# A two-layer hybrid decoder trunk on one core: where the conditioning products, the head norm, the low part and the spatial products stand in the order of work

## The chip, the cores and the metric

The kernel runs on one core of one Trainium2 chip. The metric is the device time of one execution in microseconds (us). The engines are TensorE (PE in the profile; its weight loads are PEld), VectorE (DVE), ScalarE (ACT), GpSimd (POOL) and SyncE (SP), which here issues nearly all DMAs from one queue, in program order.

## The reference

The input is x (256 tokens by 1024) and one conditioning vector c of 1024. Two layers follow, each of three sub-layers: a SwiGLU FFN (inner size 2816), a token mixer, a second FFN. The mixer of layer 0 is HGRN2, a gated linear recurrence with 8 heads of 128 in chunks of 64; the mixer of layer 1 is a gMLP with spatial gating over chunks of 128 tokens.

```python
def sublayer(x, fn, pre_g, post_g, shift, scale, gate, res_w):
    h = rms_norm(x, pre_g) * (1.0 + scale) + shift
    return x + res_w * gate * rms_norm(fn(h), post_g)

cond = silu(c)
mod = (cond @ ada_w[i] + ada_b[i]).reshape(B, 9, D_MODEL)   # shift, scale, gate of 3 sub-layers

def swiglu(h, w_in, w_out):
    a, b = split(h @ w_in, 2)
    return (silu(a) * b) @ w_out

# HGRN2: q, f, i, g = split(h @ w_in); log-decays b = cumsum(log f) in a chunk
#   scores[t, s] = sum_k q[t,k] k[s,k] exp(b[t,k] - b[s,k]) for s <= t, and a carried state
#   out = (rms_norm over each head(o) * out_norm * silu(g)) @ w_out
# gMLP: u, v = split(gelu(h @ w_in + b_in)); v = layer_norm(v)
#   out = (u * (tril(w_s[group]) @ v + b_s)) @ w_out
```

All is float32. The weights are some 280 MB that are read once.

## The kernel before

**Products in three parts.** Every weight block is read as float32, split into a high part (`hi`, a float32r cast on ACT, L122) and a low part (`lo` = raw - hi, a subtraction on DVE, L132), and activations are split in the same way; a product is hi*hi + hi*lo + lo*hi on PE. A block is 128 x 2048 and comes in two halves of 512 KB. `cast()` issues the half's load on SP and its cast on ACT, `sub()` its subtraction on DVE, `halves(n)` n of both. The halves land in a ring of four buffers (`raw`); a load waits on SP until the subtraction four halves earlier has freed its buffer. `next_block()` (called `nb`) hands out the next finished block and keeps `ahead` more finished.

**Conditioning products.** The 144 rows of conditioning weights (128 x 1024, 512 KB each) are not multiplied on PE: `ada()` loads one and multiplies and sums it against `cond` in one DVE instruction (L192). `pace(upto, blocks)` spreads the products that a stage owes evenly over so many weight blocks: after each block, `wblock()` adds `rate` to a credit and calls `ada` once for each whole credit. Loads go into a ring of three buffers, so the load of row j waits on SP for the product of row j - 3. Before, the load of row i + 2 is issued when product i is.

**The order.** Outside two kinds of region the framework's scheduler sets the order on each engine at compile time, by its own estimate of times and by a priority that is the place in the program; SP keeps program order. The text of the program is thus a wish: a DVE instruction that the scheduler thinks ready may be put ahead of earlier ones. Each engine then runs its list strictly in order. `paced()` ties the first matmul of a filler piece behind a given matmul (`self.gate`). Between `open()` and `close()` (the boundaries between sub-layers) the order on PE, DVE and ACT is that of the text. `self.hold` keeps casts, subtractions and conditioning products that come after a boundary behind the boundary's last instruction on ACT and DVE.

**The boundary** (`boundary`, between sub-layer s and s + 1): the last products of y in four pieces mm(t, h) of 18 matmuls (t: half of the tokens, h: half of the columns), after each piece a square with a row sum on ACT (`square`, L235), a multiplication by the gate on DVE (L319), the root of the mean (`inv_rms`: ACT L80, DVE reciprocal L248), `residual` (DVE L255, squares of the new x on ACT, `half_mean` L242 on DVE, which needs the first of these squares), then the norm's scaling, PE transposes (L271), `h_high` on ACT (L274), `h_full` (float32 h, DVE L287 or ACT L285) and `h_low` on DVE (L293). `go(0)`, 96 matmuls of the next sub-layer on the first tokens (L429), needs h_low from its 17th matmul on, for columns 4 to 7 from the 21st. A `plan` of four numbers says how many halves are cast and subtracted ahead of mm(0,0), after mm(0,0), around the first `residual` and around the second.

**The recurrence** (`hgrn`): feature products for q and f of heads 0-3, then for 4-7 (`feat`, 96 matmuls for two blocks, PE L460 to L462), `gate_f` on ACT and DVE, and for each half of the heads an attention `attn(hb)`: a diagonal product, seven levels (span 64 down to 1), each with two subtractions (L741, L746), an exp on ACT, a multiplication (L752), 16 matmuls (L758) and a masked copy on DVE (L729), and last the products with v (L791, L793). `zip_steps` hands PE one step of filler (`tok`: 12 matmuls for v or the gate g; `outs`) after each step of the attention. While attention 1 runs, `outs` does the head norm of attention 0 (`stats`: square on ACT L806, sums L814, gating L810, and `rsqrt`, nine small dependent DVE instructions L88 to L101), scales by r (L832), transposes on PE (`turn`, L836), splits, and multiplies by the output weights.

**The gMLP** (`gmlp`): for each of 12 units of 256 columns 48 matmuls for u (`unit`), four spatial products `vps` (L1050, two for each half k of the unit, all four into one PSUM bank), per half a gelu on ACT and two DVE instructions (L1055, L1057; L1057 reads vps), then 24 output matmuls.

Of the kernel before, what the change touches and what calls it, by code (L numbers as in the profile page):

```python
# [18 lines left out]
P = 128  # L19
# [14 lines left out]
class Body:  # L34
# [144 lines left out]
    def ada(self, upto):  # L179

        nc = self.nc
        while self.ada_next < min(upto, 144):
            i = self.ada_next
            for j in range(len(self.ada_tiles), min(i + (1 if self.ring else 3), 144)):
                if self.ring and j % 3:
                    t = self.p4.tile([P, D], F32, tag="t4", name="ada")
                else:
                    t = self.adap.tile([P, D], F32, tag="ada", name="ada")
                self.load(t, self.d["ada"][j])
                self.ada_tiles.append(t)  # L190
            t = self.ada_tiles[i]
# [59 lines left out]
    def residual(self, t, yg, r, st=None):  # L251

        for h in range(2):
# [5 lines left out]
            else:  # L259
                self.square(self.x[t][:, hs], st[0], h)  # L260
        if st is not None:
            self.half_mean(st)

# [45 lines left out]
    def boundary(self, y, G, mm, cols, table, plan=(4, 2, 0, 0)):  # L309


        nc = self.nc
# [23 lines left out]
        for _ in range(plan[2]):  # L336
            self.cast()
        self.residual(0, yg, r, sx)
        for _ in range(plan[2]):
            self.sub()  # L340
# [18 lines left out]
        gated(1, 1, yg1)  # L359
        r = self.inv_rms(sy1)  # L360
        for _ in range(plan[3]):
            self.cast()
        hf = self.h_full(1, pa1, cols, scalar=True)
        self.residual(1, yg1, r, sx1)
        for _ in range(plan[3]):
            self.sub()
        self.h_low(0, 1, hf)
        w = [[self.ready.pop(0) for _ in range(2)] for _ in range(2)]
# [275 lines left out]
    def hgrn(self, hT, G_fn, pre_next, nxt, bg):  # L644
        nc, tc = self.nc, self.tc
        self.pace(bg, 14)
        state = {}
# [180 lines left out]
        def turn(hb, u, og, r):  # L828
# [5 lines left out]
            for i in range(4):  # L834
                c0 = (i % 2) * S + (i // 2) * P
                nc.tensor.transpose(ps[:, c0:c0 + P], on[:, i, :], self.ident)  # L836
            return ps
# [79 lines left out]
        def products(i):  # L917
            wo = nb()
            return [lambda k=k, t=t, h=h: self.out_mm(y[t][h], t, h, oTs[i], k, wo, k, i + k == 0, False)
                    for k in range(2) for t in range(NT) for h in range(2)]  # L920

        def outs():
            og, r = stats(0, ops[0], False)
            for u in range(2):
                split(0, u, turn(0, u, og, r))
            yield
            y.extend(self.y_banks())
            for j, op in enumerate(products(0)):
                op()
                if j == 3:  # L930
                    yield
            yield

        y = []
        zip_steps(attn(1, bank_a, ops[1]), [
            tok(lambda t, ps: nc.scalar.copy(gg[:, t, 512:], ps)), outs()], 0)
        self.table("silu_and_others")
# [24 lines left out]
    def gmlp(self, hT, G_fn, pre_next, nxt, bg):  # L962
# [72 lines left out]
        for u in range(12):  # L1035
# [6 lines left out]
            for k in range(2):  # L1042
# [6 lines left out]
                for t in range(NT):  # L1049
                    nc.tensor.matmul(vps[:, k * S + t * P:k * S + (t + 1) * P], v[j // 2][:, j % 2, t, c0:c0 + P],  # L1050
                                     ws[:, g, :], start=True, stop=True)
                self.tact(z[:, k * S:(k + 1) * S], pu[:, k * S:(k + 1) * S], AF.Gelu_apprx_tanh,
                          bias=bcol[:, c:c + 1])
# [96 lines left out]
    def run(self):  # L1150
# [8 lines left out]
        subs = ["ffn0", "hg", "ffn1", "ffn2", "gm", "ffn3"]  # L1159
        tables = {"f": "silu_and_others", "h": "silu_and_others", "g": "gelu_apprx_tanh_and_others"}  # L1160
        bgs = {"ffn0": 40, "hg": 64, "ffn1": 92, "ffn2": 120, "gm": 138, "ffn3": 144}
        for s, kind in enumerate(subs):
# [10 lines left out]
            def nxt(y, G, mm, s=s, st=st):  # L1173
# [3 lines left out]
                else:  # L1177
                    if s != 1:
                        self.open()
                    self.boundary(y, G, mm, st["cols"], tables[subs[s + 1][0]], (2, 1, 1, 1) if s == 1 else (4, 2, 0, 0))  # L1180
                    self.hT = self.h2[:, 0], self.h2[:, 1]
# [111 lines left out]
```

## Time and profile before

| what | value |
|---|---|
| median of 3 runs | 1182.11 us (1179.4 to 1184.67) |
| the profiled execution | 1184.81 us, of which the span 1183.0 us |
| mean granted TensorE clock of it | 0.983 of full speed |
| instructions | 17089 |

The span is from the first to the last instruction. A busy PE is modelled and covers small gaps, so it is read here by its idle times and their releasers, and by the granted clock of a stretch, which has two levels, 1.2 GHz (0.50) and 2.4 GHz (1.00). The stages lie, by the trace, at about: FFN 0 from 15 to 205 us, boundary to the recurrence to 235, recurrence to 378, boundary to 402, FFNs 1 and 2 to 767, boundary, gMLP to 975, FFN 3 to the end.

### The profile page before, as it was taken

What the parts mean: (1) busy time and instruction counts of PE and PEld (TensorE: products, weight loads), DVE (VectorE), ACT (ScalarE), POOL (GpSimd) and SP (SyncE); (2) the same over time, 40 slices, a digit from 0 to 9 for tenths busy, and PEclk for the clock granted to TensorE, in tenths of its full rate; (3) what the DMA queues carried; (4) which work ended last, traced back from release to release, by engine and by line L of the source; (5) the groups of instructions that cost most, each with busy time, mean ns of one, the idle gap of its engine ahead of it and who ended that gap; (6) DMA issues with size and microseconds to landing.
All of it is one profiled execution on the core that took longest, in us unless ns stands there. A gap on an engine that the chain in (4) does not pass through costs nothing.

```text
span 1183.0 us, 17089 instructions
## 1 busy us (share of the span) xinstructions
PE 1141.4 (96%) x6518; PEld 995.8 (84%) x6518; DVE 904.7 (76%) x1379; ACT 666.3 (56%) x1046; POOL 6.8 (1%) x16
## 2 busy tenths in 40 slices
PE   7999999999969899999999999999999999999997
PEld 6989997898867788888888888888988988888886
DVE  6987867789987699886599986567887776866742
ACT  6554536769545665556566555555754367654631
POOL 0000000000000000000000000000000000000000
PEclk9999999998979899999999999999999999999999
DMA  9889988296255299887279988426777673766720
GB/s 351 309 315 334 334 286 274 82 356 223 95 183 186 87 344 366 320 309 228 93 257 367 342 313 278 151 81 230 279 265 247 241 248 104 241 230 223 237 101 36
DMA packets 79764, 282.31 MB, mean 239 GB/s; under 512 B 9873, under 2 KB 10561, under 8 KB 79682
## 3 DMA queue, kind: packets, MB, share of 16 engines
q1 hardware_dynamic: 78626, 278.05, 67.3%
q0 software_dynamic: 1056, 3.17, 0.9%
q8 instruction: 51, 0.84, 0.3%
q14 instruction: 31, 0.25, 0.1%
HBM read 280.11 MB, written 1.07 MB: 238 GB/s over the span
## 4 chain that ended last, share of the span: by engine, by line
PE 84%; DMA 5%; DVE 5%; ACT 3%; issue 1%; SPq 0%; DVEq 0%; ACTq 0%
PE ups L454 17%; PE pps L429 9%; PE ups L455 9%; PE y L163 8%; PE y L164 8%; PE y L162 8%; PE ups L574 4%; PE ups L462 3%; PE ups L460 3%; PE ups L461 3%; DMA ada<-in_ada 2%; PE ab L758 2%; DVE w L132 2%; DMA raw<-in_wgmu 2%; ACT w L122 1%
## 5 line engine op out<-in xcount | busy, mean ns | idle before, releaser
L132 DVE TENSOR_TENSOR w<-raw,w 128x1024 fp32r<-128x1024 f32 x376 | 453.4, 1221 | 95.6 <-ACT w L122 90.2
L122 ACT CAST w<-raw 128x1024 fp32r<-128x1024 f32 x376 | 387.4, 1048 | 175.4 <-DMA raw<-in_wffn 89.3
L454 PE MATMUL ups<-h,w 128*128 128x512 f32 x864 | 302.4, 393 | 0.0
L455 PE MATMUL ups<-h,w 128*128 128x256 f32 x864 | 242.1, 280 | 0.0
L192 DVE CUSTOM_DVE_ANT_0 ada<-ada,cond 128x1024 f32<-128x1024 f32 x144 | 174.1, 1219 | 24.9 <-DMA ada<-in_ada 24.9
L454 PEld LDWEIGHTS ups<-h,w 128*128 128x128 f32 x864 | 161.8, 187 | 36.9 <-issue 0.3
L162 PE MATMUL y<-w,t 128*128 128x512 f32 x448 | 178.8, 401 | 0.0
L163 PE MATMUL y<-w,t 128*128 128x512 f32 x448 | 177.3, 396 | 1.0 <-DVE w L132 1.0
L164 PE MATMUL y<-w,t 128*128 128x512 f32 x448 | 177.0, 396 | 0.0
L455 PEld LDWEIGHTS ups<-h,w 128*128 128x128 f32 x864 | 163.2, 189 | 1.0
L429 PE MATMUL pps<-w,h 128*128 128x512 f32 x480 | 116.7, 400 | 3.1 <-DVE h L293 3.1
L460 PE MATMUL ups<-h,w 128*128 128x256 f32 x416 | 118.6, 285 | 0.0
L462 PE MATMUL ups<-h,w 128*128 128x256 f32 x416 | 117.8, 283 | 0.0
L461 PE MATMUL ups<-h,w 128*128 128x256 f32 x416 | 117.6, 283 | 0.0
L429 PEld LDWEIGHTS pps<-w,h 128*128 128x128 f32 x480 | 91.0, 192 | 22.5 <-DVE h L293 3.5
L164 PEld LDWEIGHTS y<-w,t 128*128 128x128 f32 x448 | 84.3, 188 | 20.3
L163 PEld LDWEIGHTS y<-w,t 128*128 128x128 f32 x448 | 84.5, 189 | 19.2 <-DVE w L132 1.5
L162 PEld LDWEIGHTS y<-w,t 128*128 128x128 f32 x448 | 84.5, 189 | 18.8
L460 PEld LDWEIGHTS ups<-h,w 128*128 128x128 f32 x416 | 79.7, 192 | 1.1 <-issue 0.2
L461 PEld LDWEIGHTS ups<-h,w 128*128 128x128 f32 x416 | 79.7, 191 | 0.8 <-issue 0.2
L462 PEld LDWEIGHTS ups<-h,w 128*128 128x128 f32 x416 | 79.6, 191 | 0.0
L80 ACT ACTIVATE t<-t 128x256 f32<-128x256 f32 (+2 forms) x70 | 36.4, 522 | 45.4 <-DVE t L507 33.5
(198 smaller groups left out, 1317.1 us busy)
## 6 DMA issues: line engine op xcount, KB each, us to landing
raw<-in_wffn SPq DMA_DIRECT2D x264, 512.0 KB, 5.7
ada<-in_ada SPq DMA_DIRECT2D x144, 512.0 KB, 6.8
raw<-in_wgmu SPq DMA_DIRECT2D x48, 512.0 KB, 5.3
raw<-in_whg SPq DMA_DIRECT2D x40, 512.0 KB, 5.7
raw<-in_wgmv SPq DMA_DIRECT2D x24, 512.0 KB, 4.9
G<-gflat POOLq DMA_DIRECT2D x6, 512.0 KB, 5.8
t<-in_gbin SPq DMA_DIRECT2D x6, 256.0 KB, 5.7
x<-in_x SPq DMA_DIRECT2D x2, 512.0 KB, 4.2
```

What stands on the lines that cost most here:

```text
L122: self.after(self.nc.scalar.copy(hi[:, sl], raw), self.hold[0])
L132: self.after(self.nc.vector.tensor_sub(lo[:, sl], raw, hi[:, sl]), self.hold[1])
L162: self.paced(mm(ps, l[0], r[0], start=start, stop=False))
L163: mm(ps, l[0], r[1], start=False, stop=False)
L164: mm(ps, l[1], r[0], start=False, stop=stop)
L192: self.after(nc.vector.tensor_tensor_reduce(t, t, self.cond, 1.0, 0.0, ALU.mult, ALU.add, self.mod[i // 24][:, i % 24:i % 24 + 1]), self.h ...
L429: lambda g=g, i=i, j=j, kc=kc, w=w: mm(res[g][t], h2[:, i, t, kc, :], w, start=kc + i + j == 0, stop=i == 1 and kc == KC - 1)))
L454: self.paced(mm(ps, u[0], self.h2[:, :, :, kc, :], start=kc == 0, stop=False))
L455: self.last = mm(ps[:, 1, :], u[1], self.h2[:, 0, :, kc, :], start=False, stop=kc == KC - 1)
L460: self.paced(mm(o, u[0], h[0], start=start, stop=False))
L461: mm(o, u[0], h[1], start=False, stop=False)
L462: self.last = mm(o, u[1], h[0], start=False, stop=stop)
```

## The change

Five places change. (1) `ada` loads one row ahead of the product in place of two, in the same three buffers (except in the first eight blocks of FFN 0, which are not touched). (2) In the recurrence the 24 conditioning products are spread over 8 blocks in place of 14: three to a block. With the blocks that the boundary takes, these eight are handed out before attention 0 begins in the text. (3) The boundary's `half_mean` of the second residual moves behind `h_low`, the scalar `h_full` ahead of the casts and `h_low` ahead of the subtractions; the plan of boundary 0 goes from (4, 2, 0, 0) to (0, 2, 1, 3), that of boundary 1 from (2, 1, 1, 1) to (3, 1, 1, 0). (4) The head norm of attention 0 (`stats`) becomes a step of its own, ahead of the gate's filler, with a priority 400 places earlier; `outs` keeps the rest and so comes one step later, and the transposes are tied by `paced`. (5) The four spatial products of a unit are issued ahead of its four DVE instructions and two gelus.

```diff
--- before.py
+++ after.py
@@ -181,7 +181,7 @@
         nc = self.nc
         while self.ada_next < min(upto, 144):
             i = self.ada_next
-            for j in range(len(self.ada_tiles), min(i + (1 if self.ring else 3), 144)):
+            for j in range(len(self.ada_tiles), min(i + (1 if self.ring else 2), 144)):
                 if self.ring and j % 3:
                     t = self.p4.tile([P, D], F32, tag="t4", name="ada")
                 else:
@@ -258,8 +258,6 @@
                 self.load(self.out[t][:, hs], self.x[t][:, hs])
             else:
                 self.square(self.x[t][:, hs], st[0], h)
-        if st is not None:
-            self.half_mean(st)
 
     def h_high(self, t, h, xn, cols):
 
@@ -336,6 +334,7 @@
         for _ in range(plan[2]):
             self.cast()
         self.residual(0, yg, r, sx)
+        self.half_mean(sx)
         for _ in range(plan[2]):
             self.sub()
         r = self.inv_rms(sx)
@@ -358,13 +357,14 @@
         sq(1, 1, sy1)
         gated(1, 1, yg1)
         r = self.inv_rms(sy1)
+        hf = self.h_full(1, pa1, cols, scalar=True)
         for _ in range(plan[3]):
             self.cast()
-        hf = self.h_full(1, pa1, cols, scalar=True)
         self.residual(1, yg1, r, sx1)
+        self.h_low(0, 1, hf)
         for _ in range(plan[3]):
             self.sub()
-        self.h_low(0, 1, hf)
+        self.half_mean(sx1)
         w = [[self.ready.pop(0) for _ in range(2)] for _ in range(2)]
         self.res, go = self.proj(w)
         r = self.inv_rms(sx1)
@@ -643,7 +643,7 @@
 
     def hgrn(self, hT, G_fn, pre_next, nxt, bg):
         nc, tc = self.nc, self.tc
-        self.pace(bg, 14)
+        self.pace(bg, 8)
         state = {}
         self.ahead = 2
         H4 = 1024
@@ -833,7 +833,7 @@
             ps = self.acc.tile([P, 512], F32, tag="acc", name="ots")
             for i in range(4):
                 c0 = (i % 2) * S + (i // 2) * P
-                nc.tensor.transpose(ps[:, c0:c0 + P], on[:, i, :], self.ident)
+                self.paced(nc.tensor.transpose(ps[:, c0:c0 + P], on[:, i, :], self.ident))
             return ps
 
         def split(hb, u, ps):
@@ -919,10 +919,14 @@
             return [lambda k=k, t=t, h=h: self.out_mm(y[t][h], t, h, oTs[i], k, wo, k, i + k == 0, False)
                     for k in range(2) for t in range(NT) for h in range(2)]
 
+        def norm():
+            with tc.high_priority(offset=400):
+                state["norm"] = stats(0, ops[0], False)
+            yield
+
         def outs():
-            og, r = stats(0, ops[0], False)
             for u in range(2):
-                split(0, u, turn(0, u, og, r))
+                split(0, u, turn(0, u, *state["norm"]))
             yield
             y.extend(self.y_banks())
             for j, op in enumerate(products(0)):
@@ -933,7 +937,7 @@
 
         y = []
         zip_steps(attn(1, bank_a, ops[1]), [
-            tok(lambda t, ps: nc.scalar.copy(gg[:, t, 512:], ps)), outs()], 0)
+            norm(), tok(lambda t, ps: nc.scalar.copy(gg[:, t, 512:], ps)), outs()], 0)
         self.table("silu_and_others")
         g_silu(1)
         pre_next()
@@ -1049,6 +1053,9 @@
                 for t in range(NT):
                     nc.tensor.matmul(vps[:, k * S + t * P:k * S + (t + 1) * P], v[j // 2][:, j % 2, t, c0:c0 + P],
                                      ws[:, g, :], start=True, stop=True)
+            for k in range(2):
+                c = 2 * u + k
+                g = c // 3
                 self.tact(z[:, k * S:(k + 1) * S], pu[:, k * S:(k + 1) * S], AF.Gelu_apprx_tanh,
                           bias=bcol[:, c:c + 1])
                 shift = self.bcp.tile([P, P], F32, tag="bc", name="bc")
@@ -1158,6 +1165,7 @@
         self.start()
         subs = ["ffn0", "hg", "ffn1", "ffn2", "gm", "ffn3"]
         tables = {"f": "silu_and_others", "h": "silu_and_others", "g": "gelu_apprx_tanh_and_others"}
+        plans = {0: (0, 2, 1, 3), 1: (3, 1, 1, 0)}
         bgs = {"ffn0": 40, "hg": 64, "ffn1": 92, "ffn2": 120, "gm": 138, "ffn3": 144}
         for s, kind in enumerate(subs):
             res_w = 1.0 if kind in ("hg", "gm") else 0.5
@@ -1177,7 +1185,7 @@
                 else:
                     if s != 1:
                         self.open()
-                    self.boundary(y, G, mm, st["cols"], tables[subs[s + 1][0]], (2, 1, 1, 1) if s == 1 else (4, 2, 0, 0))
+                    self.boundary(y, G, mm, st["cols"], tables[subs[s + 1][0]], plans.get(s, (4, 2, 0, 0)))
                     self.hT = self.h2[:, 0], self.h2[:, 1]
 
             if kind == "hg":
```

## Rows read from the trace of the kernel before

**Rows 1.** The page's first part: busy time of each engine, share of the span and instructions.

```profile
PE 1141.4 (96%) x6518; PEld 995.8 (84%) x6518; DVE 904.7 (76%) x1379; ACT 666.3 (56%) x1046; POOL 6.8 (1%) x16
```

**Rows 2.** Who waited for whom, over the whole span: engine, line, what it waited for, us in total, times, longest.

```profile
DVE ada L192 <- DMA ada<-in_ada: 24.9, 10, 6.7
...
PE ots L836 <- DVE t L832: 10.2, 2, 8.8
...
PE vps L1050 <- DVE t L1057: 5.1, 4, 1.8
...
PE pps L429 <- DVE h L293: 3.1, 1, 3.1
...
PE npa L271 <- DVE be L242: 3.0, 2, 2.7
...
PE ab L758 <- ACT t L80: 2.7, 1, 2.7
...
PE ab L793 <- DVE t L729: 1.4, 1, 1.4
```

**Rows 3.** Stretches in which TensorE's granted clock stood at half, behind a wait. Columns: stretch, its us, PE busy (matmuls), PEld, DVE, ACT, POOL, granted clock, DMA share, GB/s.

```profile
207.50:210.80 3.30, 3.29 (x12) 2.90 (x13) 1.21 (x4) 1.93 (x6) 0.00 (x0) 0.51 0.42 164
...
279.70:285.90 6.20, 6.15 (x29) 6.15 (x30) 6.20 (x13) 6.20 (x18) 0.00 (x0) 0.50 0.57 185
...
346.60:354.10 7.50, 7.47 (x30) 6.92 (x31) 6.82 (x15) 6.30 (x8) 0.00 (x0) 0.50 0.69 236
...
364.40:367.80 3.40, 3.40 (x19) 3.40 (x17) 2.75 (x5) 1.53 (x2) 0.00 (x0) 0.50 0.61 199
...
396.10:401.90 5.80, 5.75 (x14) 4.55 (x15) 1.78 (x3) 1.66 (x2) 0.00 (x0) 0.50 0.53 168
```

**Rows 4.** The recurrence in order of time, DVE and PE, around the head norm of attention 0: start us, us, engine, line, operation, tiles, [idle before <- releaser]. The first and last of the small chain, the first of four conditioning products that stand in it, and PE.

```profile
336.27 0.16 DVE L817 TENSOR_SCALAR ss<-ss 128x8 f32<-128x8 f32 x1
...
337.77 1.22 DVE L192 CUSTOM_DVE_ANT_0 ada<-ada,cond 128x1024 f32<-128x1024 f32 x1
...
345.97 0.16 DVE L101 SCALAR_TENSOR_TENSOR r<-rs_q,rs_y 128x8 f32<-128x8 f32 x1
...
346.63 1.94 PE L836 MATMUL ots<-ident,t 128*128 128x128 f32 x8 [8.84 <-DVE t L832]
```

**Rows 5.** DVE and the others by stretch of the recurrence (columns as in rows 3).

```profile
226.40:250.00 23.60, 23.60 (x165) 22.14 (x164) 18.08 (x27) 11.90 (x17) 0.00 (x0) 1.00 0.74 269
250.00:277.00 27.00, 27.00 (x227) 26.85 (x225) 27.00 (x47) 24.18 (x39) 0.00 (x0) 1.00 0.88 303
277.00:322.00 45.00, 42.19 (x280) 38.85 (x280) 43.12 (x67) 32.64 (x64) 1.08 (x2) 0.92 0.44 145
322.00:372.00 50.00, 39.02 (x219) 34.63 (x218) 41.17 (x80) 22.56 (x28) 0.00 (x0) 0.83 0.51 169
```

**Rows 6.** The conditioning products alone (line 192; two records to a product) by stretch: us, DVE busy (records), granted clock, DMA share, GB/s.

```profile
226.40:250.00 23.60, 8.50 (x15) 1.00 0.74 269
250.00:277.00 27.00, 8.35 (x14) 1.00 0.88 303
...
322.00:346.00 24.00, 7.24 (x12) 0.88 0.42 137
sum 133.00, DVE 28.92; mean DVE 5.78
```

**Rows 7.** Loads: the page's part 6 (source, count, KB each, median us from issue to landing), and the fastest 5 us of the feature products (columns as in rows 3).

```profile
ada<-in_ada SPq DMA_DIRECT2D x144, 512.0 KB, 6.8
...
240.00:245.00 5.00, 5.00 (x44) 5.00 (x44) 2.76 (x3) 2.48 (x3) 0.00 (x0) 1.00 1.03 414
```

**Rows 8.** The filler at the end of attention 0: the stretch between the last level's matmuls and the products with v, for the filler alone (us, PE busy, PEld, DVE, ACT, clock, DMA share, GB/s), and the masked copy that the products wait for.

```profile
315.90:318.20 2.30, 2.25 (x9) 1.62 (x9) 0.00 (x0) 0.58 (x1) 1.00 0.23 39
...
316.80 1.32 DVE L729 COPY_PREDICATED t<-lmask,ab 128x512 f32<-128x512 int32 x1
```

**Rows 9.** Boundary 0 in order of time on ACT and PE: a cast that waits for its half, the square of the second piece behind it, the transposes of the first tokens.

```profile
201.12 1.05 ACT L122 CAST w<-raw 128x1024 fp32r<-128x1024 f32 x1 [0.71 <-DMA raw<-in_whg]
202.08 0.58 ACT L235 ACTIVATE junka<-y 128x512 bf16<-128x512 f32 x1
...
207.51 1.12 PE L271 MATMUL npa<-ident,xn 128*128 128x128 f32 x4 [2.65 <-DVE be L242]
```

**Rows 10.** Boundary 1 in order of time: second residual, h_full, subtraction, h_low, PE.

```profile
391.75 1.42 DVE L255 SCALAR_TENSOR_TENSOR x<-yg,r,x 128x512 f32<-128x512 f32 x2
392.08 1.49 ACT L285 ACTIVATE hf<-npa,shift,A 128x128 f32<-128x128 f32 x4
...
394.28 1.22 DVE L132 TENSOR_TENSOR w<-raw,w 128x1024 fp32r<-128x1024 f32 x1
...
395.41 0.68 DVE L293 TENSOR_TENSOR h<-hf,h 128x512 fp32r<-128x512 f32 x1
...
396.15 0.80 PE L429 MATMUL pps<-w,h 128*128 128x512 f32 x1 [3.06 <-DVE h L293]
```

**Rows 11.** One unit of the gMLP in order of time: a conditioning row's load on SP, its product, and the next spatial products on PE, which wait for the DVE instruction that reads vps.

```profile
872.93 0.42 SPq L57 DMA_DIRECT2D ada<-in_ada  x1
...
880.04 1.23 DVE L192 CUSTOM_DVE_ANT_0 ada<-ada,cond 128x1024 f32<-128x1024 f32 x1 [3.50 <-DMA ada<-in_ada]
...
882.86 0.38 PE L1050 MATMUL vps<-w 128*128 128x128 f32 x1 [1.70 <-DVE t L1057]
```

## The prediction

> **What bounds the kernel now.** I read the page's busy shares first. PE is busy for 96% of the span and DVE for 76% [rows 1], so matmuls bound the kernel, and a change that leaves their number alone can only take away PE's waits and the time in which its clock is low. The second view is the list of who waited for whom: the reader should look only for rows in which PE is the one that waits [rows 2]. They are few and short, and each has one place: the head norm of attention 0 (8.8 us in one wait), the spatial products of the gMLP (5.1 in four), the low part in boundary 1 (3.1), the transposes in boundary 0 (2.7), the first level of attention 0 (2.7), the products with v of attention 1 (1.4). The third view is the granted clock by stretch [rows 3]: behind five of these waits PE ran at half clock (1.2 GHz) for 3.3 to 7.5 us, and half of PE's busy time there is lost: 1.6, 3.1, 3.7, 1.7 and 2.9 us, 13.0 in all. Waits and clock together are some 37 us. That is the purse; FFNs 1 to 3 have nothing in it.
>
> **The change part by part.** The sum is made against the profiled execution's own 1184.81 us. A gain has a minus sign.
>
> *Head norm (early, and without conditioning products).* PE stands for 8.84 us at the transposes because r is late on DVE [rows 4]. From L817 at 336.27 to the last L101 (ends 346.13) the chain of small instructions takes 9.9 us, since each waits behind whatever the scheduler put between, four conditioning products among it. Six products in that stretch took 7.24 us [rows 6], 1.2 each, so they make up 4.8 of the 9.9. After the change all 24 belong to blocks that are handed out before attention 0, the norm is asked for at once when attention 0 ends, and the transposes come a filler step later. The strong end is the whole wait and its half clock, -12.5 (8.8 + 3.7); the weak end is only the products' share of the wait, -4.8, with the clock still falling. I take -10: nearer the strong end, because two causes of the delay go together, but other DVE work still stands between the small instructions.
>
> *Filler one step later.* The output products move behind the last level of attention 1, where PE waited 1.4 us and then ran at half clock (1.7): -2.5, from 0 to -3.1 [rows 2, 3]. The price is at the end of attention 0: nine filler matmuls of the gate ran there for 2.25 us while the masked copy ended (at 318.12) that the products with v need [rows 8]. They are now tied behind a later level. With one conditioning product less ahead of the copy I take +1.5; bounds 0 and +3.9 (2.2, and 1.7 at half clock, the shortest such stretch [rows 3]).
>
> *24 products over 8 blocks.* Together they cost 28.9 us of DVE; 16.9 of it already lie between 226.4 and 277 [rows 6], so up to 12.0 more have to go there. DVE was idle for 5.5 us up to 250 (23.6 less 18.08) and not at all from 250 to 277 [rows 5]. So 6.5 us spill over and make attention 0's first level later, where PE waits now (2.7). For it, boundary 0 ends some 3 us earlier, and what leaves the stretches after 277 gives DVE its time back: from 322 to 372 it was busy for 41.2 of 50 us, and six products there go. Bounds 0 and +8 (6.5, and 1.5 more at half clock); I take +2.5. Queued behind a late product on DVE are the subtractions of the next weight block, and PE waits for those. Loads: from 226.4 until the last feature block 16 rows and 12 halves are to be moved, 28 loads of 0.524 MB, 14.7 MB. PE reaches that block at about 269 (from 235 three groups of 96 matmuls at 0.119 us, which is 27.0 us by 227 [rows 5]). At 414 GB/s, the fastest 5 us [rows 7], the loads end at 262 and are hidden; at 303 GB/s, the mean of 250 to 277 [rows 5], at 275, which the same +8 covers.
>
> The Trainium skill, page "DMA: Bandwidth & Descriptors", section "Where 436 GB/s comes from", says that a load from HBM is limited to about 358 GB/s a core; by that the loads would end at 267.5, with a cast and a subtraction at about 270, and this term would be an estimated +3.5 in place of +2.5. The trace's 414 GB/s over 5 us lies above the page's figure, and the measurement decides.
>
> *Boundary 0.* The square of the second piece came at 202.08, behind a cast that had waited for its half (0.71) and ran for 1.05 us [rows 9]; a subtraction stood ahead of the gating in the same way. With the plan (0, 2, 1, 3) no half that has not landed stands ahead of it. I take 2.0 of PE's 2.65 us and 1.0 of the 1.6 at half clock: -3. Moved: one cast ahead of the first residual's squares and three (3.2 us on ACT) ahead of the second's. The latter are covered by the 35 matmuls of go(0), 8 us at 0.23, that PE has ahead of the next transposes; without that cover PE waits up to 3. The three halves free their buffers later, which the loads above include. Bounds -4.2 and +2.5.
>
> *Boundary 1.* PE stops for 3.06 us until h_low is done at 396.09 [rows 10]. h_low needed h_full, which ended at 393.57 and would have ended one cast (1.05) earlier, and the residual, which ended at 393.17; it stood behind half_mean (which waits for a square) and a subtraction of 1.22. Put right behind the residual it ends at 393.17 + 0.68 = 393.85: -2.2. PE's stop is then 0.8 us, and the half clock behind it (2.9) goes or stays; I take -1.8 of it: -4. Bounds -6 and 0 (the third half ahead of mm(0,0) delays the first square). At the other three boundaries PE waits for nothing that moves: 0, covered by the matmuls of go(0).
>
> *Spatial products.* The second half's two products go into the bank that L1057 reads for the first half, and in PE's list they stand behind that read: at 882.86 PE stood 1.70 us until L1057 was done, and L1057 was late because DVE had stood 3.50 us for a conditioning row [rows 11]. With all four ahead of the reads the next unit's go to another bank: -4.5 of the 5.1; bounds -5.1 and 0.
>
> *One row ahead.* It costs no instruction. On SP the load of row j waits for product j - 3, with weight halves queued behind it; one place later that product is done, so weights come no later, and rows later. DVE waited 24.9 us for rows, ten times [rows 2], and PE is named behind that only in the gMLP, which the part above takes away. I take 0; bounds 0 and +3 (half of one longest wait of 6.7 reaching PE).
>
> Sum: -10 - 2.5 + 1.5 + 2.5 - 3 - 4 - 4.5 + 0 = -20, so 1164.8 by the profiled execution. That one lies 2.7 above the median of the runs shown, 1182.11, so the same step from the median gives 1162; I predict 1163. All strong ends give -30.9 (1151 from the median), all weak ends +12.6 (1197).
>
> **The rivals.**
> - *The feature products become bound by the ring of rows, and the kernel gets slower.* With three products to a block and three buffers, the last row of each block waits for the last product of the block before. One round is a landing and a product, 6.8 + 1.2 = 8.0 us [rows 7, 4], against 5.7 us of PE for a block (48 at 0.119); eight blocks lose 18.4, and a half clock of 1.7 behind a wait in each of the four groups 6.8. In place of +2.5 that is +25: 1188 with the others unchanged (-22.5). For it: 1.7 rows to a block already took 303 GB/s. Against it: all but ten of 144 products found their row landed. It decides from +22.5 on. Chance 0.09.
> - *The head norm's wait only moves.* Its instructions, asked for early, delay the levels of attention 1 and still sit behind others: -4.8, no gain behind the last level, and the spill at its full +8: -6.8, 1178 by the profiled run and within half a per cent. For it: DVE is the full engine there. Chance 0.15.
> - *The waits shrink but the clock still falls.* Each remaining wait of a microsecond keeps its half clock: head norm -7.5, last level -1.4, boundary 0 -2, boundary 1 -2.2, first level +4: -12, 1171. For it: one wait of only 1.4 us had half clock behind it. Chance 0.18.
> - *Forecast*: 1153 to 1169, chance 0.58.
>
> **How the numbers follow.** Half a per cent (6 us) is about what a measurement of this kernel tells from no change: 1176 to 1188. Faster: the forecast, the third case and a little of the second, 0.78; same: the rest of the second and the edge of the first, 0.14; slower 0.08. The range from 1151 (all strong ends) to 1183 leaves out the slower case and little else.
>
> **What would show it.** Right: PE's wait for L832 falls under 2 us for attention 0; no half clock between 330 and 375; PE no longer waits for L1057; h_low's wait at the boundary to FFN 1 is about 1 us; no product of line 192 lies inside attention 1. Wrong: PE waits in the feature products for a subtraction or, through it, for a row; the first level's wait grows beyond 5 us; PE waits longer at the end of attention 0 than at the head norm before. The forecast falls if the scheduler puts the products, which it may move, somewhere else than the blocks that own them.

## The result, and the profile after

The changed kernel took 1188.1 us (median of 10), the kernel before beside it 1182.3: ratio 1.0045, 95% interval 1.0026 to 1.0063. The forecast was 1163; the change makes the kernel slower by 6 us. The profiled execution is the fastest of its ten, 1182.1 us (span 1180.3), so the two spans alone (1183.0 before) would tell a gain of 2.7; a second profile of the changed kernel (e1 below) lies at its median. Where the two part is told under e9.

Who waits for whom, after; columns as in [rows 2].

```profile
DVE ada L192 <- DMA ada<-in_ada: 33.0, 11, 6.2
...
PE ots L836 <- DVE t L832: 4.2, 1, 4.2
PE fps L462 <- DVE w L132: 4.0, 3, 2.9
...
PE ab L758 <- DVE rs_sh L88: 3.2, 1, 3.2
PE ab L758 <- ACT t L80: 3.0, 1, 3.0
...
PE ab L758 <- DVE t L752: 2.3, 1, 2.3
...
PE fps L460 <- ACT w L122: 2.0, 2, 1.8
PE y L162 <- ACT t L167: 1.6, 1, 1.6
PE pps L429 <- DVE be L242: 0.8, 1, 0.8
```

The 8.8 us at the head norm of attention 0, the waits for L1057 and most of the wait for h_low are gone. The 0.8 us left of it are put down to L242, which ends 0.07 us behind `h_low` on DVE. New are waits in the feature products (fps, 6.0 in all), at the second level of attention 0 (L752, 2.3), at the first level of attention 1 (3.2) and at the last unit of the gMLP (1.6); the one at the head norm of attention 1 grew (4.2, 1.4 before).

The conditioning products by stretch, then all engines; columns as in [rows 6] and [rows 5].

```profile
226.40:250.00 23.60, 11.12 (x20) 1.00 0.91 333
250.00:277.00 27.00, 10.70 (x18) 0.91 0.82 288
277.00:322.00 45.00, 5.98 (x10) 0.83 0.47 168
322.00:372.00 50.00, 0.00 (x0) 0.93 0.27 91
```

```profile
250.00:277.00 27.00, 20.80 (x153) 19.01 (x151) 26.63 (x43) 20.59 (x33) 0.00 (x0) 0.91 0.82 288
...
322.00:372.00 50.00, 46.34 (x290) 41.69 (x289) 38.99 (x71) 24.77 (x38) 0.50 (x1) 0.93 0.27 91
```

The products left attention 1, as meant: PE is busy for 46.3 of its 50 us, 39.0 before. The price is one stretch earlier: from 250 to 277 PE is busy for 20.8 of 27, and all 27 before [rows 5].

The clock, in the stretches of [rows 3] and in the new ones.

```profile
200.00:226.00 26.00, 25.39 (x120) 20.68 (x119) 20.72 (x38) 22.56 (x48) 0.00 (x0) 1.00 0.37 133
...
271.90:282.10 10.20, 7.04 (x29) 6.45 (x30) 9.21 (x13) 4.36 (x6) 0.00 (x0) 0.50 0.93 309
285.50:292.30 6.80, 5.71 (x26) 5.71 (x27) 6.78 (x12) 6.11 (x17) 0.00 (x0) 0.50 0.92 363
...
333.30:340.10 6.80, 6.80 (x29) 6.32 (x28) 4.30 (x15) 2.92 (x7) 0.00 (x0) 0.50 0.00 0
...
396.10:401.90 5.80, 5.05 (x23) 3.84 (x22) 4.60 (x11) 5.47 (x16) 0.00 (x0) 1.00 0.00 0
```

Both boundaries keep the full clock now (the transposes of boundary 0 come at 203.2, h_low's products at 400.1). The recurrence lost it for longer: around three waits of the feature products within 7 us (2.9, 1.8 and 0.5) it stood at 1.2 GHz for 10.2 us, in 7.0 of which PE was busy, and again behind the first level of attention 0 (285.5) and of attention 1 (333.3).

**Where the time went, by stage.** Each number is the distance between the first matmuls of two groups, read from the traces. Start: first feature product. A: from there to the first level of attention 0. B: to the second level of attention 1. C: to its last level. D: to the transposes at the end of FFN 1. Start + A + B + C + D is the time of those transposes ("sum"); FFN 2 adds the same everywhere (except with 13 weight tiles). The stages come from one profiled execution of each kernel. Runs are compared by the ratio to the kernel before that ran beside them, since its own median lay between 1180.8 and 1183.5 us. These letters are stages; those of the theories below are not.

| kernel | start | A | B | C | D | sum | median | ratio to before |
|---|---|---|---|---|---|---|---|---|
| before | 234.8 | 44.9 | 47.0 | 33.4 | 217.7 | 577.8 | 1182.3 | |
| after | 229.8 | 56.8 | 55.1 | 22.2 | 215.3 | 579.2 | 1188.1 | 1.0045 [1.0026, 1.0063] |
| e1 after again | 229.9 | 56.8 | 55.1 | 22.2 | 215.5 | 579.5 | 1187.0 | 1.0055 [1.0034, 1.0076] |
| e2 14 blocks | 230.2 | 45.7 | 52.7 | 26.8 | 213.4 | 568.8 | 1179.0 | 0.9972 [0.9953, 0.9990] |
| e3 no norm step | 230.1 | 57.0 | 50.7 | 22.3 | 210.8 | 570.9 | 1177.7 | 0.9979 [0.9962, 0.9995] |
| e4 four row buffers | 231.3 | 57.4 | 49.4 | 22.1 | 228.3 | 588.6 | 1213.5 | 1.0269 [1.0242, 1.0297] |
| e5 neither | 230.0 | 45.7 | 48.0 | 34.4 | 211.1 | 569.2 | 1174.7 | 0.9942 [0.9920, 0.9964] |
| e6 no row loads | 229.8 | 54.3 | 49.7 | 22.1 | 216.6 | 572.5 | 1180.4 | 1.0000 [0.9980, 1.0020] |
| e7 short products | 231.6 | 51.2 | 55.7 | 22.1 | 217.1 | 577.7 | 1180.4 | 0.9993 [0.9977, 1.0010] |
| e8 two ahead | 232.5 | 62.6 | 52.9 | 22.1 | 217.3 | 587.5 | 1191.3 | 1.0073 [1.0055, 1.0092] |
| e9 pairs again | 230.1 | 57.2 | 55.1 | 22.2 | 215.5 | 580.1 | 1186.7 | 1.0039 [1.0021, 1.0056] |
| e10 eight rows to FFN 0 | 233.8 | 47.9 | 45.9 | 22.7 | 210.9 | 561.2 | 1169.2 | 0.9882 [0.9866, 0.9897] |
| e11 neither, two ahead | 231.4 | 45.1 | 48.2 | 31.6 | 211.1 | 567.4 | 1176.3 | 0.9927 [0.9897, 0.9956] |
| e12 13 weight tiles | 231.2 | 57.0 | 56.1 | 22.1 | 228.4 | 594.8 | 1218.0 | 1.0289 [1.0271, 1.0308] |
| e13 no loads, short | 230.0 | 43.3 | 51.7 | 22.1 | 215.5 | 562.7 | 1169.5 | 0.9911 [0.9890, 0.9933] |
| e14 four rows to FFN 0 | 230.1 | 55.5 | 46.4 | 22.7 | 211.3 | 566.1 | 1172.3 | 0.9923 [0.9901, 0.9944] |

After less before: -5.0 (boundary 0), +11.9 (A), +8.1 (B), -11.2 (C), -2.4 (D), in all +1.4 at the end of FFN 1. C holds the head norm of attention 0, and it gave about what was forecast; A and B took it back. D is -5.0 at boundary 1 and +2.6 ahead of it. The norm step also moves twelve matmuls of filler, 2.8 us at 0.23, out of B into C, so the two stages are best read together. By the medians the loss is 5 to 6 us, by the stages 1.4 to 1.7: the rest is not located. The profiled execution of before lies some 2.5 above its median, and three profiles with the new order (after, e1, e9) agree within 0.9 at the end of FFN 1 while their whole times differ by 4.8, so most of it lies behind FFN 2.

### The profile page after: what moved, and what is told of

Same layout as the page of the kernel before. It is cut to its first block, busy times and chain, and to the rows that moved or that the text cites. A ratio compares the mean times of both kernels' runs of the same rounds, so it can differ in the third digit from the quotient of the medians.

```text
span 1180.3 us, 17103 instructions
## 1 busy us (share of the span) xinstructions
PE 1141.9 (97%) x6518; PEld 997.0 (84%) x6518; DVE 904.6 (77%) x1379; ACT 665.9 (56%) x1046; POOL 6.8 (1%) x16
## 4 chain that ended last, share of the span: by engine, by line
PE 77%; DVE 9%; DMA 8%; ACT 4%; issue 2%; SPq 0%; DVEq 0%; ACTq 0%
PE ups L454 17%; PE ups L455 9%; PE y L164 8%; PE y L162 8%; PE y L163 8%; PE pps L429 7%; PE ups L574 4%; DVE w L132 3%; DMA ada<-in_ada 3%; DMA raw<-in_wgmu 2%; PE ups L460 2%; PE ups L462 2%; PE ups L461 2%; PE ab L758 2%; ACT w L122 2%
## 5 line engine op out<-in xcount | busy, mean ns | idle before, releaser
L429 PE MATMUL pps<-w,h 128*128 128x512 f32 x480 | 113.9, 393 | 0.8 <-DVE be L242 0.8
```

Of the source, the lines that this page charges most:

```text
L429: lambda g=g, i=i, j=j, kc=kc, w=w: mm(res[g][t], h2[:, i, t, kc, :], w, start=kc + i + j == 0, stop=i == 1 and kc == KC - 1)))
```

## The experiments

The first theories: R, the ring of three row buffers paces the feature products; N, the early norm and the later filler push attention 1 back; D, DVE is full.

**e1, the changed kernel again.** 

> The changed kernel once more, nothing edited, for a second profile and the spread. Theory R (the ring of rows: with three products to a block and three buffers, the last row of each block waits for the last product of the block before, a round of 8 us against 5.7 us of TensorE): 1186 to 1190, TensorE waits in the last two feature groups and at the first levels of attention 0 again, 8 to 12 us behind the kernel before there. Theory N (the early head norm and the filler that comes a step later displace attention 1): the same time, but the loss against before arises after the first level of attention 1.

Measured 1187.0. The loss is there again, and every stage agrees with after within 0.2 us.

**e2, 14 blocks again.**

```diff
-        self.pace(bg, 8)
+        self.pace(bg, 14)
```

> The changed kernel with the recurrence's 24 products over 14 blocks again; all else as changed. R: the feature products lose their waits, attention 0 starts on time, the gains of the two boundaries and of the gMLP (about 4 + 4 + 4 us) stay: 1170 to 1176, ratio about 0.992. N: the loss lies in attention 1 and stays, with products in it again: 1186 to 1192.

**e3, the head norm back in `outs`.**

```diff
-                self.paced(nc.tensor.transpose(ps[:, c0:c0 + P], on[:, i, :], self.ident))
+                nc.tensor.transpose(ps[:, c0:c0 + P], on[:, i, :], self.ident)
...
+            og, r = stats(0, ops[0], False)
...
-            norm(), tok(...), outs()], 0)
+            tok(...), outs()], 0)
```

> The changed kernel with the head norm back in its old step (no step of its own, no priority, transposes not tied), the products still over 8 blocks. R: the loss of the feature products stays; the norm's wait of 8.8 us shrinks by the products that no longer lie in it (4.8) but stays in part: 1186 to 1192. N: the displaced attention 1 is gone: 1176 to 1182.

e2 measured 1179.0, 3 above what R expected and far from N; e3 measured 1177.7, as N expected and not R. Either edit undone gives back some 9 us, so neither theory alone can stand. The question became whether the two edits do the same work twice.

**e5, both undone** (the diffs of e2 and e3 together).

> The changed kernel with 14 blocks for the 24 products again and with the head norm inside the output step again; boundary, spatial products and one row ahead stay. Theory T (two cures for one wait): either edit alone takes away the wait of 8.8 us at the head norm, each has a price of its own of 9 to 10 us, and together both prices are paid for one gain; with neither, the wait is back and both prices are gone: 1176 to 1182 us, ratio 0.995 to 1.0, PE waits 8 to 10 us at the first transposes of the recurrence. Theory A (each edit simply costs 9 us, whatever the other does): 1166 to 1172 us, ratio about 0.985.

Measured 1174.7, between the two expectations. The wait is back, as theory T had it:

```profile
PE ots L836 <- DVE t L832: 10.3, 2, 8.8
```

The four kernels (both edits, each alone, neither) settle it by stage. The 24 rows over 8 blocks, with e5 as the base, cost 11.3 in A and 2.7 in B and give 12.1 in C. The norm step costs 4.7 in B and 2.3 in D and gives 7.6 in C. Both together give 12.2 in C, no more than the rows alone, and pay every price. At the end of FFN 1 that is -0.4 for the norm step, +1.7 for the rows, +10.0 for both; by the ratios +3.5, +4.4 and +12 to +13 us. So theory T holds in its mechanism, two cures for one wait; the prices that it named (9 to 10 us each) were too high: alone, the rows pay 14.0 in A and B and get 12.1 back in C, the norm step pays 7.0 in B and D and gets 7.6. In e3 the wait is gone with no norm step at all:

```profile
PE ots L836 <- DVE t L832: 1.2, 1, 1.2
```

(the one wait that is left is attention 1's). The norm step's price in B, in the trace of after, DVE, ACT and PE at the first level of attention 1:

```profile
329.02 0.69 DVE L814 TENSOR_REDUCE ss<-t 128x4 f32<-128x512 f32 x1 [0.40 <-ACT t L806]
329.63 0.68 DVE L810 TENSOR_TENSOR t<-ab,w 128x512 f32<-128x512 f32 x1
330.23 0.68 DVE L741 TENSOR_TENSOR t<-w 128x512 f32<-128x512 f32 x1
330.82 0.68 DVE L814 TENSOR_REDUCE ss<-t 128x4 f32<-128x512 f32 x1
331.42 0.68 DVE L810 TENSOR_TENSOR t<-ab,w 128x512 f32<-128x512 f32 x1
...
332.09 0.68 DVE L752 TENSOR_TENSOR t<-t,w 128x512 f32<-128x512 f32 x1
...
332.92 0.29 PE L758 MATMUL ab<-t 128*128 128x64 f32 x1 [3.22 <-DVE rs_sh L88]
```

The sums (L814) and gatings (L810) of the norm stand ahead of L741 and L752, which make the operands of the level that PE waits for: 3.2 us, and then 6.8 us at half clock. (The wait is put down to L88, the norm's next small instruction, which starts right behind L752.) The price in D, at the head norm of attention 1:

```profile
374.13 1.04 ACT L122 CAST w<-raw 128x1024 fp32r<-128x1024 f32 x1 [1.22 <-DMA raw<-in_wffn]
...
375.21 1.23 DVE L132 TENSOR_TENSOR w<-raw,w 128x1024 fp32r<-128x1024 f32 x1 [0.45 <-ACT w L122]
376.35 0.17 DVE L817 TENSOR_SCALAR ss<-ss 128x8 f32<-128x8 f32 x1
...
377.68 0.66 PE L836 MATMUL ots<-ident,t 128*128 128x128 f32 x2 [4.18 <-DVE t L832]
```

L817 stands on DVE behind the subtraction of a half of FFN 1 whose load landed late: its cast had waited 1.2 us for it.

**e4, four row buffers, and e12, its control.**

```diff
-        self.whl = pool("whl", 14)
+        self.whl = pool("whl", 13)
-        self.adap = pool("adap", 3)
+        self.adap = pool("adap", 4)
```

> The changed kernel with four buffers for the conditioning rows in place of three (and 13 in place of 14 weight tiles, to make room for it). R: the last row of a block no longer waits for the last product of the block before, the round falls to about the loads' own time (five loads of 0.524 MB, 6.3 us at 414 GB/s): feature products lose 0.6 us a block in place of 2.3, 8 to 12 us faster than the changed kernel: 1176 to 1181. N: no change, 1186 to 1190. A third theory, D (the DVE is full there and the ring does not matter): within 3 us of the changed kernel, and the first level of attention 0 still late.

Measured 1213.5, which no theory gave: the fourth buffer was paid for with a weight tile. e12 has that tile less and three buffers:

> The changed kernel with 13 weight tiles in place of 14 and three row buffers: a control for the run with four row buffers, which paid for the fourth with a weight tile. If the tile is what cost 26 us there: 1205 to 1215 us, with waits of 5 to 6 us at the transposes of the last boundaries. If the fourth row buffer cost it: 1186 to 1190 us.

Measured 1218.0, 3 above its expectation: the tile cost some 30 us (waits of up to 5.6 us at the boundaries' transposes). The fourth buffer gave at most a little back: the ratios, 1.0269 and 1.0289, overlap; by stage it is 6.2 us, all of it in B (49.4 against 56.1) and none in A (57.4 against 57.0). A looser ring alone does not free the feature products.

**e6, no row loads in the recurrence, and e7, short products.**

```diff
-                self.load(t, self.d["ada"][j])
+                if not 40 <= j < 64:
+                    self.load(t, self.d["ada"][j])
```

(e6: the product then reads `cond` in place of the row; e7: loads as they were, and for these rows `t[:, :64]` and `cond[:, :64]`.)

> The changed kernel with the 24 conditioning rows of the recurrence not loaded (the products run as long as before on a row that is there already; the sums they give are not the reference's). No product waits for a row, no load waits for a product. Theory R (the ring of three buffers sets the pace of the feature products): the waits in the feature products go, the first level of attention 0 starts at 273 to 277 us, in all 1170 to 1176 us. Theory D (DVE is full, the products themselves stand ahead of what PE needs): the first level still starts at 283 to 288 us, in all 1182 to 1188 us.

> The changed kernel with the 24 products of the recurrence over 64 columns in place of 1024 (all loads and the ring stay; the sums are not the reference's). Theory D (DVE is full): 24 products of 1.2 us become some 0.2 us each, the first level starts at 271 to 276 us, in all 1166 to 1174 us. Theory R (the ring): a round is still a landing of 6.3 to 6.8 us against 5.7 us of PE for a block, so about half of the loss stays: the first level at 279 to 283 us, in all 1179 to 1184 us.

Both took 1180.4, and A fell only to 54.3 and 51.2. The first level of attention 0 came at 284.1 and 282.8 (286.6 in after): in e6 where theory D had it, in e7 where theory R had it, so each run speaks for the cause that it left in. For e6, who waits from 228 to 300 (lines of the kernel stand two further down), and the engines from 250:

```profile
PE ab L760 <- DVE gate L219: 12.1, 1, 12.1
```

```profile
250.00:270.00 20.00, 20.00 (x170) 20.00 (x169) 20.00 (x36) 15.96 (x29) 0.00 (x0) 1.00 0.25 88
270.00:285.00 15.00, 2.91 (x21) 2.71 (x21) 15.00 (x29) 10.53 (x21) 0.00 (x0) 0.72 0.54 178
```

No feature product waits any more, DVE is busy for every one of the 35 us, and the first level waits for 12.1 behind it. For e7, the same two views (one line further down):

```profile
PE ab L759 <- DVE t L753: 3.5, 1, 3.5
PE fps L463 <- DVE w L132: 2.7, 4, 1.6
PE fps L461 <- ACT w L122: 2.1, 1, 2.1
```

```profile
250.00:270.00 20.00, 19.16 (x155) 18.34 (x153) 13.51 (x32) 15.95 (x29) 0.00 (x0) 1.00 0.86 295
270.00:285.00 15.00, 10.89 (x66) 10.27 (x67) 9.83 (x26) 11.73 (x23) 0.00 (x0) 0.77 0.96 344
```

DVE is idle for a third of the time, and the feature products wait for casts and subtractions of halves that come late behind the rows. Each cause was there without the other.

**e13, both cuts.**

> Both cuts together: the 24 rows of the recurrence are not loaded and their products are over 64 columns (the sums are not the reference's). Theory B (two limits side by side: with the loads gone DVE still holds the first level up, with the products short the loads still do, and only both together give the time back): the first level of attention 0 starts at 272 to 277 us, in all 1165 to 1173 us. Theory O (neither is the cause; the order that the scheduler gives the instructions, or the boundary's plan, is): the first level stays at 281 to 285 us, in all 1178 to 1182 us.

Measured 1169.5, A 43.3: 13.5 us less than after, where the single cuts gave 2.5 and 5.6. The first level comes at 273.3, as theory B expected. From 228 to 300 PE waits only for (lines three further down)

```profile
PE ab L761 <- DVE t L755: 1.8, 3, 1.3
PE fps L465 <- DVE w L132: 0.2, 1, 0.2
```

Theory B holds: two limits side by side, DVE and the loads. One reserve: the scheduler sees other durations in e6, e7 and e13 and may order DVE a little differently, which these runs can't split off. B and D are 51.7 and 215.5 here, against 48.0 and 211.1 in e5: the norm step's price, with no row in sight.

The ring itself shows on SP in after, the groups of three row loads:

```profile
237.24 3.24 SPq L57 DMA_DIRECT2D ada<-in_ada  x3
...
244.95 3.05 SPq L57 DMA_DIRECT2D ada<-in_ada  x3
...
252.91 3.22 SPq L57 DMA_DIRECT2D ada<-in_ada  x3
```

A round is 7.7 and 8.0 us, the 8.0 of the first rival, against 5.7 of PE. From 226 to 290 SP waits for products, which free the buffers, for nearly twice as long as before (before, then after):

```profile
SPq L57 <- DVE mod L192: 25.7, 12, 5.7
...
SPq L57 <- DVE mod L192: 49.3, 18, 11.8
```

But the rival's sum, a landing and a product, is not what makes the round: in e7, with products of 0.2 us, it is as long.

```profile
244.77 2.64 SPq L57 DMA_DIRECT2D ada<-in_ada  x3
...
252.75 2.10 SPq L57 DMA_DIRECT2D ada<-in_ada  x3
```

There the next block's first product stands on DVE behind a subtraction that waits 1.8 us for its cast on ACT (251.35): the round goes through the weight halves, and the product's own time matters little. Nor is it shown that the ring, and not the rate of the loads, sets the round: five loads of 0.524 MB in 7.7 us are 340 GB/s, the DMA engines of e7 are busy for 96% from 270 to 285, and the fourth buffer of e4 gave nothing in A.

**e8, rows two ahead again.**

```diff
-min(i + (1 if self.ring else 2), 144)
+min(i + (1 if self.ring else 3), 144)
```

> The changed kernel with rows loaded two ahead again. If one row ahead costs nothing (the prediction's term): 1186 to 1190 us, ratio about 1.005. If later rows hold up DVE, which waits 33.0 us for rows after the change and 24.9 before: 1180 to 1185 us, and PE's waits at the end of the gMLP are gone too.

**e11, the same on e5.**

> As the run with neither of the two edits (14 blocks, norm inside the output step), and with rows loaded two ahead again: only the boundaries' order and plan and the grouped spatial products of the change are left. If one row ahead is worth 4 us on its own: 1177 to 1180 us, and the transposes of boundary 0 come 2 to 3 us later. If it is worth something only with three rows to a block: 1173 to 1176 us.

e8 took 1191.3: both expectations had it that going back costs nothing or helps, and it costs some 3 us (ratio 1.0073 against 1.0045 to 1.0055, intervals that overlap); by stage it is clearer, 2.7 at the start of the features and 5.8 in A, of which part comes back later. e11 took 1176.3, between its two expectations: the start is 1.4 later and A is no longer; the ratios of e5 and e11 overlap. One row ahead is a gain where the rows are dense, and at most a small one at boundary 0.

**e9, spatial products in pairs again.**

```diff
-            for k in range(2):
-                c = 2 * u + k
-                g = c // 3
```

> The changed kernel with the spatial products of the gMLP two by two again; all else stays. If the grouping is worth what was forecast (4.5 us): 1191 to 1194 us. If the time won in the units is given back at the last one, where PE in the changed kernel waits for the cast of the gated values behind casts of weight halves that have not landed: 1186 to 1189 us, the four waits for L1057 are back and the wait at the last unit is gone.

Measured 1186.7, against 1188.1 and 1187.0: the grouping is worth nothing, as the second theory had it. The waits for L1057 are back (its line is L1061 here, 3.8 us in five) and the last unit's is gone:

```profile
PE vps L1054 <- DVE t L1061: 3.8, 5, 1.8
```

That last unit in e5, where the wait is longest:

```profile
958.71 1.04 ACT L122 CAST w<-raw 128x1024 fp32r<-128x1024 f32 x1 [2.41 <-DMA raw<-in_wffn]
...
960.51 1.28 ACT L74 ACT_TABLE_LOAD   x1
961.80 0.62 ACT L167 CAST t<-t 128x512 fp32r<-128x512 f32 x1
...
962.48 0.80 PE L162 MATMUL y<-w,t 128*128 128x512 f32 x1 [3.87 <-ACT t L167]
```

ACT holds the cast of the gated values (L167) behind that of a half of FFN 3 that has not landed, and behind the load of a function table, 1.3 us. The units come sooner, the weights don't. The length of this wait changes from one execution to the next: 1.6 us in the profile of after, 4.1 in two waits in e1's, and most of the 4.8 us between these two executions lies in that sub-layer (from the first spatial product to the next boundary 136.6 and 140.2 us, 140.8 before).

**e10, eight rows to FFN 0, and e14, four.** Both on e3, 8 blocks:

```diff
-        bgs = {"ffn0": 40, "hg": 64, ...
+        bgs = {"ffn0": 48, "hg": 64, ...
```

> The changed kernel with the head norm inside the output step again and with 8 of the recurrence's 24 conditioning rows taken by FFN 0 (48 rows there in place of 40), so that 16 are spread over the recurrence's first 8 blocks, two to a block. Theory F (the front of the recurrence is full: DVE and the ring are both at their limit at three to a block): its price falls from 10 us to 0 to 3, the wait at the head norm stays away since no product lies in it: 1163 to 1170 us, first level of attention 0 at 276 to 279 us. Rival: two to a block are still too many, or FFN 0 has no room for eight more: 1174 to 1180 us, like the run with the norm undone.

> As the run with eight rows moved to FFN 0, but four: 20 rows over 8 blocks, 2.5 to a block. Theory F (the front's price grows with the rows that it holds): the first level of attention 0 lies between that run's 281.7 and the 287.1 us of the run with 24 rows and the norm undone, at 282 to 285 us less what boundary 0 gains, 1170 to 1175 us in all. Rival (a step: two to a block fit and anything above pays the whole price): 1176 to 1179 us.

e10 is the version that beats both: 1169.2 us, ratio 0.9882. With two rows to a block A is 47.9 (57.0 with three), B 45.9, and C keeps the whole gain. It pays 3.7 us at boundary 0 (start 233.8), which e14, with four rows moved, does not; e10's first level comes at 281.7, later than the 276 to 279 of theory F, and still waits 5.7 us for DVE (L752). e14 took 1172.3, the time that theory F gave, but by another way: at 2.5 rows to a block A is already 55.5, close to the price of three, and the gain over e3 lies in B (46.4). So A is nearly a step between 2 and 2.5, as the rival had it. Part of it is the later start of e10: by the clock of the span the first level comes at 281.7, 285.7 and 287.1 with 2, 2.5 and 3 rows. The rate of the loads alone could make such a step, by an estimate: two halves and 2, 2.5 or 3 rows of 0.524 MB in the 5.7 us of a block are 368, 414 and 460 GB/s, and the fastest 5 us of the feature products moved 414 [rows 7]. No run splits this from the ring, and why B is shorter is not shown.

## Why the prediction was wrong

- **24 products over 8 blocks: the step that failed.** Put at +2.5 with bounds 0 to +8; it measured +11.3 in A and 2.7 in B (e3 against e5). The sum took one limit at a time. DVE's overflow, 6.5, was nearly right (6.0 us of products lie behind 277), but 4.0 were taken off it for boundary 0's earlier end and the DVE time that comes free later; e6, with DVE alone in the way, has A 8.6 above e5. And the loads were taken as hidden as soon as their bytes fitted, and the ring was made a rival with the chance 0.09. Its round of 8.0 us was met, but not by its sum (e7); and its 1188 us is the measured time by luck, since it put the front at +25 and left the other gains whole, where the front cost 14 and gains elsewhere failed. With loads and DVE both at their limit, freeing one leaves half of the loss or more.
- **Head norm: right in size, wrong in cause.** C gave -11.2 where -10 was forecast. The weak end, only the products' share of 4.8, was taken for the least that the rows' leaving could give; e3 shows that it gives all 12.1. The same gain would have come without the norm step.
- **The early norm was costed at nothing.** Its own work on DVE ahead of attention 1's first level was only mentioned in the second rival, without a price. It is 4.7 or 4.4 in B and 2.3 or 4.5 in D (e2 against e5, after against e3). The +1.5 for the end of attention 0 shows no wait to speak of: PE waits 0.4 us for the masked copy.
- **Last level: wrong.** Its wait and half clock are gone, but PE then stands for 4.2 us at the head norm of attention 1, which is late on DVE behind a half of FFN 1 (e5 above), and 3.4 us at half clock follow. From the last level to the transposes of boundary 1 it is 26.6 us before and 29.2 after: +2.6 where -2.5 was forecast.
- **Boundary 0: right in kind.** -5.0 at the first feature product against -3, more than the strong end of -4.2; e8 and e11 put 1.4 to 2.7 of it on one row ahead.
- **Boundary 1: right.** From its transposes to those at the end of FFN 1 it is 191.1 before and 186.1 or 186.2 in every run with the new order and 14 weight tiles: -5.0 against -4. The wait fell from 3.1 to 0.8 as worked out.
- **Spatial products: wrong.** The four waits went, but -4.5 became 0; the sum followed the wait to its end and not the weights that set when the sub-layer can end.
- **One row ahead: wrong in sign.** 0 to +3 was said; it is a gain of some 3 us with three rows to a block (e8), shown by the stages more than by the ratios.
- **Signs:** four of the five that were to show it right came (no wait for L832 in attention 0, none for L1057, 0.8 us at h_low, no product in attention 1); the fifth did not, since half clock stands from 333.3 to 340.1. The first that was to show it wrong came too: feature products that wait for a subtraction; the other two did not (3.0 us at the first level, 0.4 at the end of attention 0).
- **The sum.** From -20 to +6 it is 26 us. By stage 17 of them lie up to the end of FFN 1: the rows cost 11.5 more than was put and the norm step 7 to 9, less what the boundaries and the head norm gave beyond their terms. 4.5 are the spatial products, and some 4 more are not located. (Of the two ends of that sum, 1151 is counted from the median and 1197 from the profiled execution; from the median the second is 1195.)
- **Load rate.** The prediction let the loads end at 262, by the 414 GB/s of the fastest 5 us. Over the 24 us in which the front loads, e2 moved 357 GB/s with the DMA engines busy for 95%; at the start of FFN 0 the changed kernel moved 400 over as long:

```profile
226.00:250.00 24.00, 24.00 (x186) 23.26 (x185) 20.64 (x35) 12.97 (x19) 0.00 (x0) 1.00 0.95 357
...
11.00:35.00 24.00, 21.59 (x162) 21.35 (x161) 19.93 (x36) 14.91 (x22) 0.00 (x0) 0.93 1.02 400
```

The rate of 5 us did not hold over the front. The Trainium skill, page "DMA: Bandwidth & Descriptors", section "Where 436 GB/s comes from", gives about 358 GB/s a core for loads from HBM; the 357 of the front agrees with it, the 400 lies above it. The term that the prediction worked out from the page's figure, an estimated +3.5, still falls far short of 14.0.

## What to carry to other kernels

Before two edits are added up, ask whether they remove the same wait: the gain counts once, and both prices are paid. When work is packed into a shorter stretch, put it against every resource there at once (here DVE, and the loads with their ring and queue); with two of them full, easing one gave back 5 to 7 of some 16 us by the ratios (e6, e7 and e13 against after), and moving a third of the work to an earlier stage (e10) was worth more than any edit of the order tried here. A stall ahead of a point that waits for loads is partly free: follow the time that is won to the next load before counting it.

## What the runs showed that was not expected

Around three waits in the feature products, none above 2.9 us and with matmuls between them, the clock stood at 1.2 GHz for 10.2 us, of which PE was busy for 7.0; before, single waits of 2.7 us were followed by 3.3 (boundary 0) and 6.2 (first level), and one of 3.1 by 5.8 [rows 2, 3]. A wait's length alone thus does not tell how long the clock stays low. A program of 14 weight tiles loses some 30 us with one tile less (e12), more than any edit here won.
